# Attention scores in a two-layer decoder trunk: heads paired over the array's two row halves, masks added on VectorE

## The chip, the cores and the metric

The kernel runs on one core of one Trainium2 chip. The metric is device time in microseconds, the median of several runs. The kernel before takes 1220.24 us (three runs, 1218.81 to 1221.25).

## What is computed

The reference is a two-layer decoder trunk on x of shape (1, 256, 1024) in float32. Each layer is a half SwiGLU block, a token mixer, cross-attention into 256 memory tokens, and another half SwiGLU block, each with its RMS norm and residual. What matters here are the scores of the token mixers. All heads have 64 dimensions, and the 256 tokens are two blocks of 128.

```python
# layer 0, band heads (8 query heads, 2 key heads): scores, distance bias, band mask, a sink in the softmax
s = einsum(q, k) * dh ** -0.5
s = where(valid, s + bias, -inf); m = maximum(max(s), sink)
p = exp(s - m); o = (p / (sum(p) + exp(sink - m))) @ v
# layer 0, stick-breaking heads (8): no softmax
z = einsum(q, k) * scale
log_keep = where(strict, log_sigmoid(-z), 0)
a = where(strict, exp(log_sigmoid(z) + cumsum_after(log_keep)), 0); o = a @ v
# layer 1, dilated heads (16): three dilation patterns mixed, which one softmax does
# over s + bias, where the bias holds the slope and the log of how often a key counts
```

## The kernel before, in words

The program is one stream written in order: for each layer FFN, mixer, cross-attention, FFN. Nearly all work on TensorE (PE) is matrix products of activations with weights. Each weight tile is loaded from HBM by SP's queue (`raw`, L170 and L172), rounded to a high part on ScalarE (`wh`, L174) and subtracted to a low part on VectorE (`wl`, L176), and each product is then three matmuls (`mm3`, L181 to L183; in the FFN's wide form L318 and L319). The pools hold 4 raw tiles, 10 tiles of weight parts (five pairs), 10 work tiles of 128x512 (`wk`), 6 PSUM banks for products (`mm`) and 2 for transposes (`tp`).

The small work of attention is put between those products by a planner in Python. `later(delay, fn)` puts a step on a heap with a due time; each product calls `tick(ns)` with its supposed cost, which advances the planner's clock and then starts at most one step that is due. A step's own tick advances the clock too, but starts nothing. `need(tag)` starts all steps of that tag that are left. The delays stand in `LAG`. The framework then schedules the instructions by priority (the order written) and readiness, so an instruction can move past one that would not be ready, and it gives each tile a free buffer of its pool; an engine runs its queue in the order so made.

Three places make scores:

- **Band heads**, `even_mixer`'s `scores` (L572) called from `attend` (L443). Groups are of four heads for the first block of queries (128 keys) and of two heads for the second (256 keys), six groups: (0,0), (0,4), (1,0), (1,2), (1,4), (1,6). Heads 0 to 3 lie on partitions 0 to 63 of `qaT` and `kaT`, heads 4 to 7 on partitions 64 to 127. Each head's slice of the bank gets the bias table by a bfloat16 matmul with an identity over all 128 rows (L580), and then the product of 64 rows (L582, float32, which runs as two passes of weight load and matmul). VectorE reduces the maxima from PSUM (L587, L589), ScalarE makes the exponentials from PSUM into a work tile (L455), 7.5 us of the planner later four transposes (L207) and a copy (L461) follow, and then the products with values (L603). Between these steps stand the products that make the stick-breaking queries and keys (`ws_blocks`, L306).
- **Stick-breaking heads**, `stick(h)` (L674), one head after another with a gap of 1900 ns. A bfloat16 matmul over all rows writes the mask of 384 columns (L679); two float32 products of 64 rows with 256 and 128 columns are added to it (L680, L682). Even heads lie on the lower half of the partitions, odd heads on the upper half. ScalarE makes abs, exp and log (L686 to L688), VectorE and ScalarE the parts of the log sums (L692 to L697), and 3200 ns of the planner after the scores `after` sums them on PE (L704 to L706); then L708, L709, and 1000 ns later the products with values (L717 to L719). Between these steps stands the projection of the memory's keys (`mem.keys`, 96 matmuls of 512 columns).
- **Dilated heads**, `odd_mixer`'s `scores` (L786), twelve groups: four of four heads with 128 keys, then eight of two heads with 256 keys. Each group loads its bias table into a work tile (L794), makes products of 64 rows (L800), and VectorE adds bank and table in place (L804). Then come L807, L455 and, 17.6 us of the planner later, the transposes. All heads of one group lie on one half of the partitions (`hf`). The projection of the values and of the memory's keys stand between.

Of the kernel before, what the change touches and what calls it, by code (L numbers as in the profile page):

```python
# [13 lines left out]
BF16 = mybir.dt.bfloat16  # L14
AF = mybir.ActivationFunctionType
ALU = mybir.AluOpType
AX = mybir.AxisListType

P = 128
# [19 lines left out]
def kernel(  # L39
# [95 lines left out]
    ident_b = const.tile([P, P], BF16, name="ident_b")  # L135
    nc.vector.tensor_copy(ident_b, ident)
# [10 lines left out]
    def psum():  # L147
        return mm.tile([P, 512], F32, name="mm")
# [371 lines left out]
    def even_mixer(w_in, q_gain, k_gain, sinks, w_out, next_vec, mem, first=False):  # L520
# [18 lines left out]
        def evac_qk(t, pq, pk):  # L539
# [17 lines left out]
            def turn():  # L557
# [5 lines left out]
                if t == 1:  # L563
                    attend([(0, 0), (0, 4), (1, 0), (1, 2), (1, 4), (1, 6)], scores, values, LAG['band_gap'], LAG['band_p'],
                           first=1500.0, tag="band")
# [5 lines left out]

        def scores(grp):  # L572
# [3 lines left out]
            ps = psum()  # L576
            for i in range(per):
                hf, b = (h0 + i) // 4, (h0 + i) % 4
                sl = ps[:, i * keys:(i + 1) * keys]
                nc.tensor.matmul(sl, lhsT=ident_b, rhs=bband[:, h0 + i, 2 * P - keys:2 * P],  # L580
                                 start=True, stop=False)
                nc.tensor.matmul(sl, lhsT=qaT[hf * 64:(hf + 1) * 64, b, t * P:(t + 1) * P],  # L582
                                 rhs=kaT[hf * 64:(hf + 1) * 64, 0:keys], start=False, stop=True)
            tick(1100)
            s = blocks(ps, keys)
# [5 lines left out]
            return s, nm, dn[t][:, h0:h0 + per], None  # L591
# [81 lines left out]

        def stick(h):  # L674
            hs = slice((h % 2) * 64, (h % 2) * 64 + 64)
            b = h // 2
            ps = psum()
            z = ps[:, 0:384]
            nc.tensor.matmul(z, lhsT=ident_b, rhs=smask, start=True, stop=False)  # L679
            nc.tensor.matmul(ps.rearrange("p (a t) -> p a t", t=256)[:, :, 0:128],  # L680
                             lhsT=kbT[hs, b, 0:P], rhs=qbT[hs, b, :], start=False, stop=False)
            nc.tensor.matmul(ps[:, 128:256], lhsT=kbT[hs, b, P:2 * P], rhs=qbT[hs, b, P:2 * P],  # L682
                             start=False, stop=True)
            tick(830)
# [53 lines left out]
    def odd_mixer(w_in, q_gain, k_gain, w_out, next_vec, mem):  # L738
# [45 lines left out]

        if True:
            def scores(grp):  # L786
# [6 lines left out]
                tab = work()  # L793
                nc.sync.dma_start(blocks(tab, keys), dil_bias[:, h0:h0 + per, 256 - keys:256])  # L794
                ps = psum()
# [218 lines left out]
```

## Time and profile before

| | |
|---|---|
| median of three runs | 1220.24 us (1218.81 to 1221.25) |
| the profiled execution's own time | 1220.4 us |
| its span, first to last instruction | 1218.6 us |
| instructions | 17064 |
| TensorE clock granted over the span | 1.00 (2.4 GHz) |

The rows in a later section come from that one execution. PE is TensorE's matmuls, PEld its weight loads, DVE is VectorE, ACT ScalarE, POOL GpSimd, SP the engine whose queue issues the DMAs. Starts and durations in a timeline are microseconds from the first instruction; rows of like instructions next to each other are merged, with their count behind the x, and the duration is then that from the first start to the last end. A matmul's duration includes its way through the array, so matmuls overlap in the rows, and what one takes of the engine's time is read from start to start. A form like 64*128 128x256 is 64 rows by 128 columns of weights; the last number is how many columns are streamed.

### The profile page before, as it was taken

Reading aid. Unit: us, or ns where it says so; the run is one execution under the profiler, and the core shown is the slowest. Engines: PE = TensorE matmul, PEld = TensorE weight load, DVE = VectorE, ACT = ScalarE, POOL = GpSimd, SP = SyncE. Lnnn points to the kernel's source line nnn. Section 1 sums busy time; section 2 is a strip of 40 time slices with the busy share of each in tenths; the row PEclk is TensorE's granted clock in tenths of the full one; section 3 lists DMA queues with packets and bytes.
Section 4 is the critical chain, followed back from the end, with each engine's and each line's share of the span. In section 5 each row is a group of like instructions: output and inputs, shape, how many; then the busy total and the mean of one; then the engine's idle time right before and its main releaser. Section 6 shows DMA issues by size and latency. Waiting matters only on the chain.

```text
span 1218.6 us, 17064 instructions
## 1 busy us (share of the span) xinstructions
PE 1209.0 (99%) x6390; PEld 1023.5 (84%) x6390; DVE 762.2 (63%) x979; ACT 648.1 (53%) x1078; POOL 63.8 (5%) x123
## 2 busy tenths in 40 slices
PE   8999999999999999999999999999999999999998
PEld 7888888887888888888888888888788888888887
DVE  6666645665766676665376675376666776667651
ACT  6656534646655565555365554265643654656540
POOL 1000000200010000000000000033000100000000
PEclk9999999999999999999999999999999999999999
DMA  8765664731444485666385657346634545665560
GB/s 261 248 193 176 220 210 136 257 107 35 138 161 143 141 272 171 195 207 207 104 259 174 207 191 263 117 155 202 204 113 139 189 145 158 222 202 178 182 199 35
DMA packets 136756, 216.71 MB, mean 178 GB/s; under 512 B 10337, under 2 KB 104161, under 8 KB 136674
## 3 DMA queue, kind: packets, MB, share of 16 engines
q1 hardware_dynamic: 136674, 215.63, 54.5%
q8 instruction: 50, 0.82, 0.3%
q14 instruction: 32, 0.26, 0.1%
HBM read 214.54 MB, written 1.05 MB: 177 GB/s over the span
## 4 chain that ended last, share of the span: by engine, by line
PE 95%; DVE 1%; DMA 1%; ACT 1%; issue 0%; POOL 0%; SPq 0%; ACTq 0%; POOLq 0%; DVEq 0%
PE mm L318 22%; PE mm L181 18%; PE mm L182 17%; PE mm L183 17%; PE mm L319 12%; PE tp L207 3%; PE mm L800 1%; DMA raw<-in_xa_w_o_dram 1%; PE mm L821 1%; DVE wl L176 1%; PE mm L582 1%; PE mm L300 1%; DMA x<-in_x_dram 0%; PE mm L603 0%; PE mm L680 0%
## 5 line engine op out<-in xcount | busy, mean ns | idle before, releaser
L176 DVE TENSOR_TENSOR wl<-raw,wh 128x1024 fp32r<-128x1024 f32 x386 | 463.7, 1220 | 145.2 <-ACT wh L174 143.8
L174 ACT CAST wh<-raw 128x1024 fp32r<-128x1024 f32 x386 | 394.0, 1051 | 156.2 <-PE mm L183 80.0
L318 PE MATMUL mm<-xs,wh 128*128 128x512 f32 x1184 | 413.7, 394 | 0.0
L319 PE MATMUL mm<-xs,wl 128*128 128x256 f32 x1184 | 331.8, 280 | 0.0
L318 PEld LDWEIGHTS mm<-xs,wh 128*128 128x128 f32 x1184 | 221.8, 187 | 50.4
L319 PEld LDWEIGHTS mm<-xs,wl 128*128 128x128 f32 x1184 | 223.8, 189 | 0.0
L181 PE MATMUL mm<-wh,big 128*128 128x512 f32 x480 | 193.3, 403 | 0.0
L183 PE MATMUL mm<-wh,big 128*128 128x512 f32 x480 | 187.4, 390 | 0.0
L182 PE MATMUL mm<-wl,big 128*128 128x512 f32 x480 | 187.3, 390 | 0.0
L181 PE MATMUL mm<-wh,xs 128*128 128x512 f32 (+1 forms) x432 | 171.9, 398 | 0.0
L182 PE MATMUL mm<-wl,xs 128*128 128x512 f32 (+1 forms) x432 | 167.6, 388 | 0.0
L183 PE MATMUL mm<-wh,xs 128*128 128x512 f32 (+1 forms) x432 | 167.3, 387 | 0.0
L322 ACT COPY wk<-mm 128x256 f32<-128x256 f32 x148 | 55.3, 374 | 152.0 <-PE mm L319 151.6
L323 DVE TENSOR_TENSOR wk<-mm,wk 128x256 f32<-128x256 f32 x148 | 62.3, 421 | 96.9 <-ACT wk L322 96.9
L181 PEld LDWEIGHTS mm<-wh,big 128*128 128x128 f32 x480 | 90.3, 188 | 19.3 <-issue 2.0
L183 PEld LDWEIGHTS mm<-wh,big 128*128 128x128 f32 x480 | 90.1, 188 | 19.2
L182 PEld LDWEIGHTS mm<-wl,big 128*128 128x128 f32 x480 | 90.4, 188 | 15.9
L183 PEld LDWEIGHTS mm<-wh,xs 128*128 128x128 f32 x432 | 81.2, 188 | 16.5
L181 PEld LDWEIGHTS mm<-wh,xs 128*128 128x128 f32 x432 | 81.3, 188 | 15.2 <-issue 0.3
L182 PEld LDWEIGHTS mm<-wl,xs 128*128 128x128 f32 x432 | 81.4, 188 | 14.3
L207 PE MATMUL tp<-ident,wk 128*128 128x128 f32 x376 | 56.7, 273 | 0.8 <-DVE wk L440 0.8
L207 PEld LDWEIGHTS tp<-ident,wk 128*128 128x128 f32 x376 | 46.0, 141 | 12.4 <-issue 1.6
(159 smaller groups left out, 959.6 us busy)
## 6 DMA issues: line engine op xcount, KB each, us to landing
raw<-in_ffn_w_gu_dram SPq DMA_DIRECT2D x344, 256.0 KB, 4.2
raw<-in_ffn_w_down_dram SPq DMA_DIRECT2D x88, 512.0 KB, 4.4
raw<-in_xa_w_kv_dram SPq DMA_DIRECT2D x32, 512.0 KB, 5.4
raw<-in_od_w_in_dram SPq DMA_DIRECT2D x24, 512.0 KB, 4.4
raw<-in_ev_w_in_dram SPq DMA_DIRECT2D x18, 512.0 KB, 4.5
raw<-in_xa_w_q_dram SPq DMA_DIRECT2D x16, 512.0 KB, 4.6
raw<-in_xa_w_o_dram SPq DMA_DIRECT2D x16, 512.0 KB, 4.3
raw<-in_ev_w_out_dram SPq DMA_DIRECT2D x8, 512.0 KB, 3.8
```

Of the source, the lines that this page charges most:

```text
L174: nc.scalar.copy(wh, r)
L176: nc.vector.tensor_tensor(wl, r, f32(wh), op=ALU.subtract)
L181: nc.tensor.matmul(ps, lhsT=a[0], rhs=b[0], start=start, stop=False)
L182: nc.tensor.matmul(ps, lhsT=a[0], rhs=b[1], start=False, stop=False)
L183: nc.tensor.matmul(ps, lhsT=a[1], rhs=b[0], start=False, stop=stop)
L207: nc.tensor.transpose(ps[:, b * P:(b + 1) * P], src[:, b * P:(b + 1) * P], ident)
L300: nc.tensor.matmul(ps[:, b * 256:(b + 1) * 256], lhsT=w[k // per][x][:, o:o + P], rhs=xboth(k)[y], start=i == 0 and k == 0, stop=i == 2 an ...
L318: nc.tensor.matmul(ps, lhsT=wh, rhs=xs[:, :, :, k, :], start=k == 0, stop=False)
L319: nc.tensor.matmul(ps[:, 0:256], lhsT=wl, rhs=xh[:, :, k, :], start=False, stop=k == NK - 1)
L322: nc.scalar.copy(part[:, bs], ps[:, 256:512])
L323: nc.vector.tensor_tensor(out[:, bs], ps[:, 0:256], part[:, bs], op=ALU.add)
L582: nc.tensor.matmul(sl, lhsT=qaT[hf * 64:(hf + 1) * 64, b, t * P:(t + 1) * P], rhs=kaT[hf * 64:(hf + 1) * 64, 0:keys], start=False, stop=True)
```

## The change

Heads are scored in pairs of groups, one group on each half of the partitions. The products of the two groups alternate between the halves, head by head, and go to two PSUM banks. A float32 product stays two passes, so passes run lower, lower, upper, upper, and so on. The pair is made when its first group comes up, and the second group then starts with the reduction. The orders of groups are changed so that partners follow each other.

For band heads the identity matmuls (16) go; VectorE adds bank and bias table into a work tile, once for each group (6 of 128x512), and the later steps read that work tile. For stick-breaking heads the mask matmuls (8) go; two heads are scored together and VectorE adds the mask, once for each head (8 of 128x384); z is then read from a work tile. For dilated heads nothing is added or removed on VectorE; the two groups' tables are loaded together. The ticks change: a pair now costs the planner 1000, 800 and 1000 ns, where two groups cost 2200, 1660 and 1780. The identity in bfloat16 goes.

```diff
--- before.py
+++ after.py
@@ -132,8 +132,6 @@
             nc.sync.dma_start(xres[t][:, cs], x_in[0, t * P:(t + 1) * P, cs])
     ident = const.tile([P, P], F32, name="ident")
     make_identity(nc, ident)
-    ident_b = const.tile([P, P], BF16, name="ident_b")
-    nc.vector.tensor_copy(ident_b, ident)
     mhalf = const.tile([P, 16], F32, name="mhalf")
     nc.gpsimd.memset(mhalf, -0.5)
     neg_1 = const.tile([P, P], F32, name="neg_1")
@@ -561,34 +559,43 @@
                 ps = transpose4(qn)
                 nc.vector.tensor_scalar(qaT[:, :, t * P:(t + 1) * P], blocks(ps), g[:, 0:1], None, op0=ALU.mult)
                 if t == 1:
-                    attend([(0, 0), (0, 4), (1, 0), (1, 2), (1, 4), (1, 6)], scores, values, LAG['band_gap'], LAG['band_p'],
+                    attend([(0, 0), (0, 4), (1, 0), (1, 4), (1, 2), (1, 6)], scores, values, LAG['band_gap'], LAG['band_p'],
                            first=1500.0, tag="band")
             later(LAG['rsband'], scale, "band")
 
         nm8 = [sm.tile([P, 8], F32, name="nm8") for _ in range(2)]
         dn = [sm.tile([P, 8], F32, name="dn") for _ in range(2)]
         po_a = [None, None]
+
+        paired = {}
 
         def scores(grp):
             t, h0 = grp
             keys = (t + 1) * P
             per = 512 // keys
-            ps = psum()
-            for i in range(per):
-                hf, b = (h0 + i) // 4, (h0 + i) % 4
-                sl = ps[:, i * keys:(i + 1) * keys]
-                nc.tensor.matmul(sl, lhsT=ident_b, rhs=bband[:, h0 + i, 2 * P - keys:2 * P],
-                                 start=True, stop=False)
-                nc.tensor.matmul(sl, lhsT=qaT[hf * 64:(hf + 1) * 64, b, t * P:(t + 1) * P],
-                                 rhs=kaT[hf * 64:(hf + 1) * 64, 0:keys], start=False, stop=True)
-            tick(1100)
-            s = blocks(ps, keys)
+            if h0 < 4:
+                two = [psum(), psum()]
+                for i in range(per):
+                    for hf in range(2):
+                        rows = slice(hf * 64, hf * 64 + 64)
+                        nc.tensor.matmul(two[hf][:, i * keys:(i + 1) * keys],
+                                         lhsT=qaT[rows, h0 + i, t * P:(t + 1) * P], rhs=kaT[rows, 0:keys],
+                                         start=True, stop=True)
+                tick(1000)
+                for hf in range(2):
+                    h = h0 + 4 * hf
+                    tab = work()
+                    nc.vector.tensor_tensor(blocks(tab, keys), blocks(two[hf], keys),
+                                            bband[:, h:h + per, 2 * P - keys:2 * P], op=ALU.add)
+                    paired[t, h] = tab
+            tab = paired[grp]
+            s = blocks(tab, keys)
             m = sm.tile([P, 8], F32, name="mx")
             nc.vector.tensor_reduce(out=m[:, 0:per], in_=s, axis=AX.X, op=ALU.max)
             nm = nm8[t][:, h0:h0 + per]
             nc.vector.scalar_tensor_tensor(nm, in0=m[:, 0:per], scalar=-1.0, in1=nsink[:, h0:h0 + per],
                                            op0=ALU.mult, op1=ALU.min)
-            return s, nm, dn[t][:, h0:h0 + per], None
+            return s, nm, dn[t][:, h0:h0 + per], tab
 
         def values(grp, pt):
             t, h0 = grp
@@ -671,17 +678,24 @@
         ob = [work() for _ in range(2)]
         po = [None]
 
+        zs = [None, None]
+
         def stick(h):
-            hs = slice((h % 2) * 64, (h % 2) * 64 + 64)
             b = h // 2
-            ps = psum()
-            z = ps[:, 0:384]
-            nc.tensor.matmul(z, lhsT=ident_b, rhs=smask, start=True, stop=False)
-            nc.tensor.matmul(ps.rearrange("p (a t) -> p a t", t=256)[:, :, 0:128],
-                             lhsT=kbT[hs, b, 0:P], rhs=qbT[hs, b, :], start=False, stop=False)
-            nc.tensor.matmul(ps[:, 128:256], lhsT=kbT[hs, b, P:2 * P], rhs=qbT[hs, b, P:2 * P],
-                             start=False, stop=True)
-            tick(830)
+            if h % 2 == 0:
+                two = [psum(), psum()]
+                rows = [slice(0, 64), slice(64, 128)]
+                for ps, hs in zip(two, rows):
+                    nc.tensor.matmul(ps.rearrange("p (a t) -> p a t", t=256)[:, :, 0:128],
+                                     lhsT=kbT[hs, b, 0:P], rhs=qbT[hs, b, :], start=True, stop=False)
+                for ps, hs in zip(two, rows):
+                    nc.tensor.matmul(ps[:, 128:256], lhsT=kbT[hs, b, P:2 * P], rhs=qbT[hs, b, P:2 * P],
+                                     start=False, stop=True)
+                tick(800)
+                for i in range(2):
+                    zs[i] = work()
+                    nc.vector.tensor_tensor(zs[i][:, 0:384], two[i][:, 0:384], smask, op=ALU.add)
+            z = zs[h % 2][:, 0:384]
             e = work()
             nc.scalar.activation(e[:, 0:384], z, AF.Abs)
             nc.scalar.activation(e[:, 0:384], e[:, 0:384], AF.Exp, scale=-1.0)
@@ -782,6 +796,8 @@
                 for fn in waiting[t]:
                     fn()
 
+        paired = {}
+
         if True:
             def scores(grp):
                 t, h0 = grp
@@ -790,18 +806,24 @@
                 per = 512 // keys
                 need(f"q{t}")
                 need(f"k{t}")
-                tab = work()
-                nc.sync.dma_start(blocks(tab, keys), dil_bias[:, h0:h0 + per, 256 - keys:256])
-                ps = psum()
-                for i in range(per):
-                    h = h0 + i
-                    hf, b = (h % 8) // 4, h % 4
-                    hs = slice(hf * 64, hf * 64 + 64)
-                    nc.tensor.matmul(ps[:, i * keys:(i + 1) * keys],
-                                     lhsT=qT[hh][hs, b * 256 + t * P:b * 256 + (t + 1) * P],
-                                     rhs=kT[hh][hs, b * 256:b * 256 + keys], start=True, stop=True)
-                tick(890)
-                nc.vector.tensor_tensor(tab, ps, tab, op=ALU.add)
+                if h0 % 8 < 4:
+                    two = [psum(), psum()]
+                    tabs = [work(), work()]
+                    for hf in range(2):
+                        h = h0 + 4 * hf
+                        nc.sync.dma_start(blocks(tabs[hf], keys), dil_bias[:, h:h + per, 256 - keys:256])
+                    for i in range(per):
+                        for hf in range(2):
+                            hs = slice(hf * 64, hf * 64 + 64)
+                            b = h0 % 4 + i
+                            nc.tensor.matmul(two[hf][:, i * keys:(i + 1) * keys],
+                                             lhsT=qT[hh][hs, b * 256 + t * P:b * 256 + (t + 1) * P],
+                                             rhs=kT[hh][hs, b * 256:b * 256 + keys], start=True, stop=True)
+                    tick(1000)
+                    for hf in range(2):
+                        nc.vector.tensor_tensor(tabs[hf], two[hf], tabs[hf], op=ALU.add)
+                        paired[t, h0 + 4 * hf] = tabs[hf]
+                tab = paired[grp]
                 s = blocks(tab, keys)
                 nm = sm.tile([P, 4], F32, name="nm")
                 nc.vector.tensor_reduce(out=nm[:, 0:per], in_=s, axis=AX.X, op=ALU.max, negate=True)
@@ -833,7 +855,7 @@
         project(lambda k: w_in[k * P:(k + 1) * P, 0:1024], xparts, evac_qk(qT, True, "q"), tags=("x0", "x1"))
         tc.keep_in_program_order(nc.scalar.preload_act_table_set("exp_and_others"))
         project(lambda k: w_in[k * P:(k + 1) * P, 1024:2048], xparts, evac_qk(kT, False, "k"))
-        groups = [(t, h) for t in range(2) for h in range(0, 16, 4 // (t + 1))]
+        groups = [(0, 0), (0, 4), (0, 8), (0, 12)] + [(1, h + o) for h in (0, 8) for o in (0, 4, 2, 6)]
         attend(groups, scores, values, LAG['att_gap'], LAG['att_p'], first=LAG['att_first'], tag="att", ready=with_v)
         project(lambda k: w_in[k * P:(k + 1) * P, 2048:3072], xparts, evac_v)
         mem.keys()
```

## Rows read from the trace of the kernel before

**Rows 1.** The page, parts 1 and 4: busy time by engine, the chain that ended last.

```profile
PE 1209.0 (99%) x6390; PEld 1023.5 (84%) x6390; DVE 762.2 (63%) x979; ACT 648.1 (53%) x1078; POOL 63.8 (5%) x123
...
PE 95%; DVE 1%; DMA 1%; ACT 1%; issue 0%; POOL 0%; SPq 0%; ACTq 0%; POOLq 0%; DVEq 0%
```

**Rows 2.** Busy time by stretch: PE, PEld, DVE, ACT, POOL, clock, DMA share, GB/s.

```profile
241.60:272.80 31.20, 31.20 (x214) 25.77 (x214) 20.56 (x34) 15.90 (x44) 0.00 (x0) 1.00 0.35 113
272.80:320.00 47.20, 47.20 (x266) 38.21 (x264) 28.84 (x52) 30.67 (x68) 2.93 (x6) 1.00 0.13 39
```

**Rows 3.** Timeline (start, us, engine, line), PE, around a first-block band group.

```profile
241.56 0.28 PE L183 MATMUL mm<-xs,wl 128*128 128x256 f32 x1
241.68 0.23 PE L580 MATMUL mm<-big,ident_b 128*128 128x128 bf16 x1
...
244.21 0.28 PE L182 MATMUL mm<-xs,wh 128*128 128x256 f32 x1
```

**Rows 4.** Timeline, PE, around one stick-breaking head.

```profile
272.60 0.39 PE L182 MATMUL mm<-wl,big 128*128 128x512 f32 x1
272.83 0.40 PE L183 MATMUL mm<-wh,big 128*128 128x512 f32 x1
...
273.33 0.70 PE L680 MATMUL mm<-big 64*128 64x256 f32 x2
273.87 0.38 PE L682 MATMUL mm<-big 64*128 64x128 f32 x2
...
274.52 0.40 PE L182 MATMUL mm<-wl,big 128*128 128x512 f32 x1
```

**Rows 5.** Timeline, PE, around a second-block band group.

```profile
252.68 0.28 PE L183 MATMUL mm<-xs,wl 128*128 128x256 f32 x1
...
254.71 0.28 PE L182 MATMUL mm<-xs,wh 128*128 128x256 f32 x1
```

**Rows 6.** Timeline, PE, around a first-block dilated group.

```profile
849.48 0.39 PE L183 MATMUL mm<-wh,xs 128*128 128x512 f32 x1
849.80 1.16 PE L800 MATMUL mm<-big 64*128 64x128 f32 x8
...
851.23 0.39 PE L182 MATMUL mm<-wl,xs 128*128 128x512 f32 x1
```

**Rows 7.** Timeline, PE, around a second-block dilated group.

```profile
870.58 0.39 PE L183 MATMUL mm<-wh,xs 128*128 128x512 f32 x1
...
872.29 0.40 PE L182 MATMUL mm<-wl,xs 128*128 128x512 f32 x1
```

**Rows 8.** Groups by line and shape: count, busy us, mean ns, idle before.

```profile
L804 DVE TENSOR_TENSOR wk<-mm,wk 128x512 f32<-128x512 f32 x12 | 8.2, 684 | 5.1 <-PE mm L800 4.2 <-DMA wk<-in_dil_bias_dram 0.9
...
L800 PEld LDWEIGHTS mm<-big 64*128 64x128 f32 x64 | 9.2, 186 | 4.7 <-issue 2.9 <-ACT wk L455 0.4 <-DVE nm L807 0.4
...
L708 DVE TENSOR_TENSOR wk<-mm,wk 128x384 f32<-128x384 f32 x8 | 4.4, 555 | 3.2 <-PE mm L706 3.2
```

**Rows 9.** Timeline, weight loads of the two dilated groups.

```profile
849.80 0.96 PEld L800 LDWEIGHTS mm<-big 64*128 64x128 f32 x8 [0.35 <-ACT wh L174]
...
870.89 0.73 PEld L800 LDWEIGHTS mm<-big 64*128 64x128 f32 x4 [0.35 <-issue]
```

**Rows 10.** Timeline, all engines, two stretches of the stick-breaking stage.

```profile
280.74 0.65 PE L207 MATMUL tp<-ident,big 128*128 128x128 f32 x4
281.02 0.56 DVE L695 TENSOR_TENSOR wk<-wk 128x384 fp32r<-128x384 f32 x1 [0.58 <-ACT wk L694]
...
282.71 0.34 PE L705 MATMUL mm<-wk,neg_ur 128*128 128x384 f32 x1
...
289.05 0.55 DVE L695 TENSOR_TENSOR wk<-wk 128x384 fp32r<-128x384 f32 x1
...
292.53 0.34 PE L705 MATMUL mm<-wk,neg_ur 128*128 128x384 f32 x1
```

**Rows 11.** Waits of SP's own queue, whole span: total us, times, longest.

```profile
SPq L794 <- PE tp L207: 12.7, 3, 10.8
```

## The prediction, as it went on record before the change was run

> **What bounds the kernel now.** I read the page's busy shares and its chain first: TensorE is busy 99% of the span and makes up 95% of the chain [rows 1]. So TensorE time that goes is gained almost in full, and work on other engines is free as long as nothing that TensorE needs comes later. Busy time by stretch says how much room there is. In the band stretch VectorE works 20.56 of 31.20 us, in the stick-breaking stretch 28.84 of 47.20, TensorE all of both [rows 2]. Then I priced each visit to the scores from start to start, since matmul durations overlap.
>
> A visit costs the time from the L183 before it to the L182 behind it, less the ordinary spacing of the two products that frame it: 0.12 us with 256 columns (241.56 to 241.68) [rows 3], 0.23 us with 512 columns (272.60 to 272.83) [rows 4].
> - band, first block, 4 heads: 244.21 - 241.56 - 0.24 = 2.41 us [rows 3]; two groups
> - band, second block, 2 heads: 254.71 - 252.68 - 0.24 = 1.79 us [rows 5]; four groups
> - stick-breaking, one head: 274.52 - 272.83 - 0.46 = 1.23 us [rows 4]; eight heads
> - dilated, first block, 4 heads: 851.23 - 849.48 - 0.46 = 1.29 us [rows 6]; four groups
> - dilated, second block, 2 heads: 872.29 - 870.58 - 0.46 = 1.25 us [rows 7]; eight groups
>
> The sum is 4.8 + 7.2 + 9.8 + 5.2 + 10.0 = 37.0 us. The change can act on no more than that, 3% of the span.
>
> **What a visit is made of.** One load takes 186 ns [rows 8]. Eight loads with 128 columns streamed take 0.96 us, so they follow each other at (0.96 - 0.19) / 7 = 0.11 us; four with 256 columns take 0.73 us, which is 0.11 for the first step and (0.73 - 0.19 - 0.11) / 2 = 0.215 for the later ones [rows 9]. So a pass costs 0.11 us at 128 columns and 0.215 at 256, and a load that nothing hides costs 0.11. The rest is fixed: 1.29 - 8 x 0.11 = 0.41, and 1.25 - 4 x 0.215 = 0.39. I take 0.40 us for leaving the full array and coming back, two ways of about 0.20; the loads' engine stands idle 0.35 us before such a visit [rows 9].
>
> **The change part by part.** *Matmuls removed and visits merged* have one price. If the two halves run strictly in turn, a pair costs 0.40 + 16 x 0.11 = 2.16 us (first block), 0.40 + 8 x 0.215 = 2.12 (second block), 0.40 + 4 x 0.215 + 4 x 0.11 = 1.70 (two stick-breaking heads). With 3, 6 and 4 such pairs that is 6.5 + 12.7 + 6.8 = 26.0 us, a saving of 11.0.
>
> *Two halves at once* has no row: nowhere before do products of the two halves stand next to each other. Bounds: no overlap saves 11.0 as above; complete overlap of the halves gives 0.40 + 0.88, 0.40 + 0.86 and 0.40 + 0.65, together 3.8 + 7.6 + 4.2 = 15.6 us, a saving of 21.4. A loss has its place under the rivals. Passes are issued lower, lower, upper, upper, so in order only the second pass of one half can lie beside the first of the other: 8 passes take 5 places, 16 take 9. The nearest row is that of the loads: they come 0.11 us apart whatever is streamed. If loads of both halves still pass one at a time, a pass of 128 columns gains nothing, since a load fills it, and one of 256 does. Then first-block pairs stay at 2.16, second-block pairs cost 0.40 + 5 x 0.215 = 1.48, stick-breaking pairs 0.40 + 3 x 0.215 + 2 x 0.11 = 1.27: 6.5 + 8.9 + 5.1 = 20.4 us. I take this value, **16.6 us saved**. If loads of both halves overlap too, first-block pairs fall to 0.40 + 9 x 0.11 = 1.39 and 18.9 us are saved.
>
> *Adds on VectorE.* Six of 128x512 at 684 ns and eight of 128x384 at 555 ns, from the nearest adds of a bank and a work tile [rows 8]: 4.1 + 4.4 = 8.5 us of VectorE, hidden under TensorE. In the band stretch VectorE then has 24.7 us in 31.2 - (12.0 - 5.1) = 24.3 us, so there it is full. The Trainium skill's page "TensorEngine Tiling (Array Packing)", section "PSUM Bottleneck", warns of this: tiling makes TensorE faster, not the emptying of PSUM, which can then be the limit. By that rule the band stretch would end 0.4 us later than my sum, no more. Without it the same follows from the rows, and the stretch behind has room: 33.2 of about 42.5 us. I count it in the term for waits.
>
> *Longer chains.* The add stands between scores and ScalarE. In the stick-breaking stage the first head's sums wait least: L695 ends at 281.58 and the matmul that reads it starts at 282.71, 1.1 us later; a later head has 292.53 - 289.60 = 2.9 us [rows 10]. In between stands the next head's visit of 1.23 us, which moves forward to the first of its pair. An add of 0.56 us and its hand-over (0.1) come in. The first head so lacks 0.8 us; later ones keep 2.9 - 1.23 - 0.7 = 1.0. For the second head of a pair the chain is shorter, its z being ready. Band groups wait 7.5 us of the planner before their transposes; dilated chains don't grow. 0.8 us is taken.
>
> *Buffers and queues.* Pairs hold z or the second table one gap longer in the 10 work tiles, but free their banks at the add. SP's queue shows that the tiles are scarce already: its table loads waited 12.7 us for transposes to release one, 10.8 us at the longest, with weight loads queued behind [rows 11]. Five pairs of weight parts cover that: each feeds four steps of three matmuls, 5 x 4 x 0.69 = 13.8 us. A pair that asks for two tiles may wait one gap more (about 5 us): 10.8 + 5 - 13.8 = 2.0 us of stall at most, nothing at least. I take 0.7, as the nearest row shows no stall. The planner's clock now moves less per pair, as TensorE does, and each stage's chain ends earlier against the filler. Tables are still 12 loads. The identity's copy at the start lies beside the first loads: nothing.
>
> **The sum.** 16.6 - 0.8 - 0.7 = 15.1 us less. The rows are of an execution of 1220.4 us with a span of 1218.6; it lies 0.16 above the median of 1220.24, and what surrounds the span stays. 1220.4 - 15.1 - 0.2 = **1205.1 us**.
>
> **Rivals.**
> *Halves in turn, no overlap.* For it: no row shows two halves at once, and the scheduler can put other work into a pair, as it put four transposes between the two products of one head [rows 10]. Against: nothing but their order links the halves. It keeps the merged visits: 1220.2 - 11.0 + 1.5 = 1210.7 us. This is also the case in which the change doesn't do what it says. Chance 0.26.
>
> *Complete overlap.* Each half would run as an array of its own, with its loads, and the order in pairs of passes would cost nothing. For it: separate rows, separate banks. Against: loads at 0.11 us each, one after another [rows 9], and queues in order. It saves 21.4: 1220.2 - 21.4 + 1.5 = 1200.3 us; with overlap in order and loads side by side 1220.2 - 18.9 + 1.5 = 1202.8. Chance of the two 0.18. The Trainium skill's page "TensorEngine Tiling (Array Packing)", section "Theoretical Speedup", gives up to twofold for a contraction of 64 rows, which is this rival's first number; no run here shows it yet.
>
> *A turn between halves costs like a change of shape (slower).* A pair of first-block groups turns 7 times, every other pair 3 times: 3 x 7 + 10 x 3 = 51 turns. If each cost a way of 0.20 us, 10.2 of the 11.0 us would go: 1220.2 - 11.0 + 10.2 + 1.5 = 1220.9, no change. If each cost leaving and entering, 0.40 us, it would be 1220.2 - 11.0 + 20.4 + 1.5 = 1231.1. It decides from (11.0 - 1.5 + 2.4) / 51 = 0.23 us per turn. For it: the full array's change to 64 rows and back is paid at every visit [rows 3, 4]. Against: both halves have one form, 64*128, and eight passes with weights of four heads pay nothing between them [rows 9]. The same page's "Key Properties" says that a change of mode drains the engine, a change of tile alone does not; by that sentence this rival falls. Chance 0.04 for no change, 0.06 for slower.
>
> *Waits eat the gain.* If full work tiles stretch the stick-breaking chain, TensorE runs out of filler. If that stage stayed at its 47.2 us [rows 2], the 9.8 - 5.1 = 4.7 us gained there would be lost: 1205.1 + 4.7 = 1209.8 us. Chance 0.04, on top of any of these.
>
> **How the numbers follow.** The forecast has 0.42, and the cases above 0.26, 0.18, 0.10 and 0.04. The time is that of the likeliest. The range goes from complete overlap (1200.3, a little less without its waits) to halves in turn with the full stall of 2.0 us (1220.2 - 11.0 + 0.8 + 2.0 = 1212.0, and 1 us for rounding in the bounds): **1199.8 to 1213.0 us**; outside are the turns that cost and a part of the rest. A difference of 0.2% (2.4 us) is about what a measurement can tell from no change. Faster by more than that: 0.87. Within: 0.06. Slower: 0.07.
>
> **What would show it.** Groups L580 and L679 are gone; 14 new adds stand on VectorE at 0.55 to 0.69 us. The visit to a second-block pair takes about 1.5 us by the same reckoning (2.1 if in turn, 1.3 if complete), a first-block pair 2.2 (1.4 if loads overlap), a stick-breaking pair 1.3. Starts of matmuls of the two halves lie close together where they overlap; a gap of 0.2 us at each turn would show the slower rival. TensorE stays at 99%; a wait of TensorE for VectorE or a work tile of over 2 us in sum would prove my terms for waits wrong, and a visit outside 1.3 to 2.2 us my account of the array.

## The result, and the profile after

The changed kernel takes 1205.74 us (median of four runs, 1204.01 to 1208.18), the kernel before 1219.93 us beside it: 0.9885 of it, with a 95% interval of 0.9863 to 0.9906. The forecast was 1205.1. The profiled execution took 1207.32 us with a span of 1205.6; against the one of before (1220.4) that is 13.1 us less.

The page's busy times and its chain by engine, changed kernel, beside [rows 1]:

```profile
PE 1192.6 (99%) x6366; PEld 1011.7 (84%) x6366; DVE 766.6 (64%) x992; ACT 646.1 (54%) x1078; POOL 63.5 (5%) x123
...
PE 92%; DVE 3%; DMA 2%; ACT 1%; issue 1%; POOL 0%; SPq 0%; ACTq 0%; DVEq 0%; POOLq 0%
```

TensorE is still the bound at 99%, but VectorE now has 3% of the chain: there are waits that were not there.

To see where time went I took landmarks, the start of the same product's last matmul in both traces (all products with weights stand in the same order): the ends of the products around the even layer's attention, around the second FFN of layer 0, and around the odd layer's attention. The two attention stretches, landmark to landmark (start:end and length, then busy us and instructions of PE, PEld, DVE, ACT and POOL, granted clock, DMA share, GB/s), before:

```profile
240.48:331.25 90.77, 90.77 (x542) 74.42 (x541) 58.67 (x95) 53.67 (x123) 3.86 (x8) 1.00 0.29 93
829.72:938.82 109.10, 109.10 (x576) 87.93 (x575) 71.60 (x93) 56.60 (x131) 12.05 (x19) 1.00 0.50 164
```

and after:

```profile
238.91:321.46 82.55, 81.74 (x518) 68.96 (x517) 64.64 (x109) 53.23 (x123) 3.95 (x8) 1.00 0.32 101
821.75:925.62 103.87, 102.19 (x577) 83.88 (x575) 70.85 (x93) 56.04 (x132) 12.05 (x19) 1.00 0.52 173
```

The even layer (band and stick-breaking) gives 90.77 - 82.55 = 8.2 us, the odd one (dilated) 5.2. The rest is not the change's: this execution reached the first landmark 1.6 us earlier, and its second FFN of layer 0 took 1.9 us more (last section).

Now the visits. TensorE's timeline, changed kernel: a band first-block pair (8 heads), a band second-block pair (4 heads) and a dilated second-block pair:

```profile
239.99 0.28 PE L181 MATMUL mm<-xs,wl 128*128 128x256 f32 x1
240.19 1.16 PE L581 MATMUL mm<-big 64*128 64x128 f32 x16
...
241.51 0.28 PE L180 MATMUL mm<-xs,wh 128*128 128x256 f32 x1
...
247.17 0.28 PE L181 MATMUL mm<-xs,wl 128*128 128x256 f32 x1
247.38 1.13 PE L581 MATMUL mm<-big 64*128 64x256 f32 x8
...
248.67 0.28 PE L180 MATMUL mm<-xs,wh 128*128 128x256 f32 x1
...
860.04 0.39 PE L181 MATMUL mm<-wh,xs 128*128 128x512 f32 x1
860.36 1.13 PE L819 MATMUL mm<-big 64*128 64x256 f32 x8
...
861.76 0.40 PE L180 MATMUL mm<-wl,xs 128*128 128x512 f32 x1
```

By the prediction's own reckoning they cost 241.51 - 239.99 - 0.24 = 1.28 us, 248.67 - 247.17 - 0.24 = 1.26 and 861.76 - 860.04 - 0.46 = 1.26. One dilated group alone cost 1.29 and 1.25 [rows 6, 7]: the second group is free. The weight loads say the same. PEld's timeline, a dilated first-block and a second-block pair:

```profile
841.83 0.97 PEld L819 LDWEIGHTS mm<-big 64*128 64x128 f32 x16 [0.35 <-ACT wh L172]
...
860.36 0.73 PEld L819 LDWEIGHTS mm<-big 64*128 64x128 f32 x8 [0.35 <-ACT big L793]
```

Sixteen loads now take the time of eight, and eight that of four [rows 9]; in the records a pass of the upper half starts 6 to 7 ns after that of the lower. All three band visits cost 3.8 us (12.0 before), all six dilated ones 7.6 (15.2 before).

The adds on VectorE, by form (line, engine, operation, tiles, count, then busy us and mean ns, then idle time before them):

```profile
L697 DVE TENSOR_TENSOR wk<-mm,smask 128x384 f32<-128x384 f32 x8 | 4.0, 547 | 0.0
...
L588 DVE TENSOR_TENSOR wk<-mm,big 128x512 f32<-128x512 f32 x6 | 3.8, 680 | 0.6 <-PE mm L581 0.6
```

They have the prices taken (684 and 555 ns). The stick-breaking pairs are another matter. TensorE's timeline, the first of them:

```profile
265.32 0.40 PE L181 MATMUL mm<-wh,big 128*128 128x512 f32 x1
265.64 0.70 PE L689 MATMUL mm<-big 64*128 64x256 f32 x2
266.27 1.10 PE L610 MATMUL mm<-big,wk 128*128 128x64 f32 x8
267.30 0.70 PE L689 MATMUL mm<-big 64*128 64x256 f32 x2
267.93 1.10 PE L610 MATMUL mm<-big,wk 128*128 128x64 f32 x8
268.96 0.49 PE L692 MATMUL mm<-big 64*128 64x128 f32 x4
...
269.73 0.40 PE L180 MATMUL mm<-wl,big 128*128 128x512 f32 x1
```

The scheduler put full-array products with values (L610) inside the pair, so the halves stand apart and the change of shape is paid three times. In the later pairs the sums of an earlier head (L718 to L720) do the same; in the fourth the second head became a visit of its own. All four are split: about 2.2, 1.9, 1.9 and 2.5 us, 8.5 in all against 9.8 before. (The work inside is taken off at what it costs elsewhere: 0.11 us a pass of L610, 0.57 us for a head's sums.)

Waits. TensorE in the odd attention stretch (line waited for, then us in total, times, longest), changed kernel:

```profile
PE mm L843 <- ACT wh L172: 0.9, 1, 0.9
PE tp L205 <- DVE wk L438: 0.7, 1, 0.7
```

The first one on VectorE's timeline and on TensorE's:

```profile
864.49 1.28 DVE L824 TENSOR_TENSOR wk<-mm,wk 128x512 f32<-128x512 f32 x2
865.69 0.67 DVE L829 TENSOR_REDUCE nm<-wk 128x2 f32<-128x512 f32 x1
866.28 0.68 DVE L459 COPY wk<-tp 128x512 f32<-128x512 f32 x1
```

```profile
867.10 1.08 PE L843 MATMUL mm<-big,wk 128*128 128x64 f32 x8 [0.86 <-ACT wh L172]
```

The rows name ScalarE's L172, but what L843 reads is the copy of the transposes, L459, which ends at 866.96. It stood on VectorE's queue behind both adds of the pair and a reduction, one add more than a single group puts there.

The second wait has one more cause in it. VectorE's timeline of that pair, from its first add to L438, which scales the attention's output before TensorE transposes it:

```profile
873.49 0.69 DVE L824 TENSOR_TENSOR wk<-mm,wk 128x512 f32<-128x512 f32 x1 [0.67 <-DMA wk<-in_dil_bias_dram]
...
877.02 0.68 DVE L438 TENSOR_TENSOR wk<-mm,rd 128x512 f32<-128x512 f32 x1
```

The first add waited 0.67 us for its bias table, and from there to the end of L438 VectorE had no pause. Ten of the eleven other traces with dilated pairs have the same: VectorE waits 0.5 to 1.1 us for that table, and TensorE then 0.5 to 2.6 us for the operation that is L438 here. In the eleventh (halves not in turn) the table is in time and TensorE still waits 0.5 us, so the late table is a part of that wait and not all of it; no run loads the tables sooner.

From start to start the odd stretch has stalls of 1.03, 0.88 and 0.29 us, the even one of 0.88 (a transpose that waits for VectorE's L188 behind the band adds) and 0.26: 3.3 us in all, 2.8 of them waits for VectorE. VectorE in the band stretch alone (columns as above), beside the first window of [rows 2], is all but full:

```profile
240.19:265.30 25.11, 24.40 (x209) 22.98 (x209) 23.65 (x44) 16.72 (x46) 0.00 (x0) 1.00 0.40 126
```

On SP's queue another table load, for a later pair, waited longest, for a work tile that L438 had to release (compare [rows 11]). TensorE lost nothing by that one: the pair's first add then waited for its products and not for a table.

```profile
SPq L814 <- DVE wk L438: 10.3, 1, 10.3
```

### The profile page after: what moved, and what is told of

Same layout as the page of the kernel before. It is cut to its first block, busy times and chain, and to the rows that moved or that the text cites. A ratio compares the mean times of both kernels' runs of the same rounds, so it can differ in the third digit from the quotient of the medians.

```text
span 1205.6 us, 17032 instructions
## 1 busy us (share of the span) xinstructions
PE 1192.6 (99%) x6366; PEld 1011.7 (84%) x6366; DVE 766.6 (64%) x992; ACT 646.1 (54%) x1078; POOL 63.5 (5%) x123
## 3 DMA queue, kind: packets, MB, share of 16 engines
HBM read 214.54 MB, written 1.05 MB: 179 GB/s over the span
## 4 chain that ended last, share of the span: by engine, by line
PE 92%; DVE 3%; DMA 2%; ACT 1%; issue 1%; POOL 0%; SPq 0%; ACTq 0%; DVEq 0%; POOLq 0%
PE mm L316 23%; PE mm L179 17%; PE mm L180 17%; PE mm L181 17%; PE mm L317 12%; PE tp L205 3%; DVE wl L174 1%; DMA raw<-in_xa_w_o_dram 1%; PE mm L843 1%; ACT wh L172 1%; PE mm L610 0%; DMA x<-in_x_dram 0%; PE mm L689 0%; DVE big L188 0%; PE mm L298 0%
## 5 line engine op out<-in xcount | busy, mean ns | idle before, releaser
L172 ACT CAST wh<-raw 128x1024 fp32r<-128x1024 f32 x386 | 394.3, 1051 | 164.6 <-PE mm L181 81.7
```

The source lines that it names most:

```text
L172: nc.scalar.copy(wh, r)
```

## The experiments

Theory: both halves run at once, their loads too; band and dilated visits give all of it, the stick-breaking part gives little because its pairs are split and its chains are longer, and VectorE's queue takes some back. Rivals: the order in turns is what makes them overlap, or the gain is that of the removed mask matmuls; and in the stick-breaking stage the due times, not the adds, are what costs. Each run is told by its ratio to the kernel before on the same chip and by the landmarks: by how much the even and the odd attention stretch of its profiled execution differ from before.

| run | median us | ratio (95%) | even, us | odd, us |
|---|---|---|---|---|
| the change | 1205.74 | 0.9885 (0.9863 to 0.9906) | -8.2 | -5.2 |
| halves not in turn | 1207.67 | 0.9895 (0.9865 to 0.9925) | -8.5 | -5.4 |
| masks on VectorE only | 1223.53 | 1.0023 (1.0013 to 1.0034) | +3.5 | 0.0 |
| dilated pairs only | 1214.63 | 0.9955 (0.9939 to 0.9972) | 0.0 | -5.0 |
| stick-breaking sums later | 1210.14 | 0.9915 (0.9894 to 0.9937) | -3.7 | -5.1 |
| dilated adds one by one | 1209.83 | 0.9913 (0.9898 to 0.9927) | -8.2 | -4.4 |
| stick-breaking as before | 1207.51 | 0.9891 (0.9874 to 0.9908) | -7.1 | -5.1 |
| pairs sooner, sums later | 1205.48 | 0.9876 (0.9859 to 0.9893) | -9.5 | -5.1 |
| the same again | 1206.91 | 0.9883 (0.9861 to 0.9906) | -9.5 | -4.9 |
| nine work tiles | 1209.96 | 0.9914 (0.9898 to 0.9929) | -4.8 | -5.2 |
| stick-breaking masks by matmul | 1203.88 | 0.9864 (0.9842 to 0.9886) | -10.7 | -5.4 |
| that, pairs sooner | 1205.53 | 0.9871 (0.9853 to 0.9890) | -10.0 | -5.3 |
| the change again | 1206.87 | 0.9884 (0.9864 to 0.9903) | -8.2 | -5.5 |

**Halves not in turn.** All products of one half, then all of the other (band, stick-breaking and dilated alike).

```diff
-                for i in range(per):
-                    for hf in range(2):
+                for hf in range(2):
+                    for i in range(per):
```

> The pairs stay, but each pair issues all products of the lower half and then all of the upper half. Theory A (the halves run at the same time when they alternate): each visit then costs the passes of both halves one after the other, 2.1 to 2.2 us for a band or dilated pair where the change takes 1.26 to 1.29, 1.7 for a stick-breaking pair that isn't split; 3 x 0.88 + 6 x 0.86 + 4 x up to 0.65 = 8 to 10 us slower than the change, about 1214 to 1216 us. Theory B (fewer visits and no mask matmuls are the gain, the order within a pair is nothing): as the change, 1205 to 1207 us.

The ratio cannot be told from the change's, so the order hardly matters to the time. TensorE's timeline of this kernel, a band first-block and a dilated second-block pair:

```profile
241.80 0.28 PE L181 MATMUL mm<-xs,wl 128*128 128x256 f32 x1
242.01 1.71 PE L581 MATMUL mm<-big 64*128 64x128 f32 x16
...
243.87 0.28 PE L180 MATMUL mm<-xs,wh 128*128 128x256 f32 x1
...
860.65 0.39 PE L181 MATMUL mm<-wh,xs 128*128 128x512 f32 x1
860.97 1.14 PE L818 MATMUL mm<-big 64*128 64x256 f32 x8
...
862.38 0.40 PE L180 MATMUL mm<-wl,xs 128*128 128x512 f32 x1
```

The 16 passes cost 243.87 - 241.80 - 0.24 = 1.83 us, between 1.28 (in turn) and 2.16 (one after another); the upper half's first pass starts at 242.57, when five of the lower half's eight have started. The 8 passes cost 862.38 - 860.65 - 0.46 = 1.27, as in turn, though all of the lower half's four were issued first. TensorE thus starts passes of the free half ahead of passes issued earlier for the busy one: three of those were passed over in either pair. Turns shorten only the long pair, and its 0.55 us show in neither stretch because the stalls were shorter in this run (the band stage's 0.33 us in place of 0.88, and none at the products with values in the odd layer).

**Masks on VectorE only.** The kernel before with the new adds of band and stick-breaking heads, no pairs.

```diff
-                nc.tensor.matmul(sl, lhsT=ident_b, rhs=bband[:, h0 + i, 2 * P - keys:2 * P],
-                                 start=True, stop=False)
...
+            tab = work()
+            nc.vector.tensor_tensor(blocks(tab, keys), blocks(ps, keys),
+                                    bband[:, h0:h0 + per, 2 * P - keys:2 * P], op=ALU.add)
...
+            zt = work()
+            nc.vector.tensor_tensor(zt[:, 0:384], ps[:, 0:384], smask, op=ALU.add)
```

> Only the masks of band and stick-breaking heads go to VectorE; no pairs, dilated heads as before. Theory A: band visits fall from 2.41 and 1.79 to about 1.28 and 1.26 us (2 x 1.13 + 4 x 0.53 = 4.4 us), stick-breaking heads from 1.23 to 1.05 (8 x 0.18 = 1.4 us), together 5.8 us less TensorE time, minus some waits: 1214 to 1216 us. Theory B: most of the 14 us is here, 1208 us or less.

Slower than before. The band visits fell as they should, to 1.28 us (four heads) and 1.25 (two heads), 7.6 us in all: 4.4 of the 8.2 us that the band part gains are the removed bias matmuls, 3.8 the pairing. But the even stretch as a whole is 3.5 us longer, so what follows the band visits lost 3.5 + 4.4 = 7.9 us. TensorE's waits in it, and the stretch that came soon after the stall of 0.8 us:

```profile
PE mm L717 <- ACT wk L709: 2.0, 1, 2.0
PE mm L704 <- ACT wk L723: 1.1, 1, 1.1
PE mm L704 <- ACT wk L694: 0.8, 1, 0.8
```

```profile
295.00:298.50 3.50, 3.50 (x10) 2.74 (x10) 1.58 (x3) 2.29 (x5) 0.00 (x0) 0.53 0.02 5
```

After a stall of 0.8 us in a stretch of small products the granted clock was 0.53 for 3.5 us (1.2 of 2.4 GHz): about half of them lost once more. Other work also split four of the eight heads' visits. VectorE was not full there (33.1 of 52.7 us, from 265.3 to 318.0). An add and a work tile per head in that chain cost more than the mask matmuls, which are worth 1.23 - 1.05 = 0.18 us a visit (a whole visit to one head cost 1.05 here). Which of the two, the add or the tile, costs more this run does not show.

**Dilated pairs only.** The kernel before with the changed `odd_mixer`.

```diff
+                if h0 % 8 < 4:
+                    two = [psum(), psum()]
+                    tabs = [work(), work()]
...
-        groups = [(t, h) for t in range(2) for h in range(0, 16, 4 // (t + 1))]
+        groups = [(0, 0), (0, 4), (0, 8), (0, 12)] + [(1, h + o) for h in (0, 8) for o in (0, 4, 2, 6)]
```

> Only the dilated heads are paired; band and stick-breaking heads as before. No matmul is removed here. Theory A: two visits of 1.28 and 1.26 us become one of the same length, so 2 x 1.28 + 4 x 1.26 = 7.6 us less TensorE time, of which the two waits of about 1 us each seen in the changed kernel are given back: 1214 to 1216 us by the time, and about 5.2 us gained between the landmarks of this stage. Theory B: six visits fewer at 0.40 us, 2.4 us minus the same waits: 1218 to 1220 us.

The odd stretch gives 5.0 us and the even one nothing: the dilated gain does not depend on the rest, and with no matmul removed it is the pairing's. Six visits fewer at 0.40 us would have given 2.4.

**Stick-breaking sums later.** 4500 instead of 3200 ns between the scores and the sums, so that no earlier head's sums are due at a pair.

```diff
-    "put": 400, "stick_gap": 1900, "stick_u": 3200, "stick_v": 1000, "stick_o": 1300, "head64": 7000,
+    "put": 400, "stick_gap": 1900, "stick_u": 4500, "stick_v": 1000, "stick_o": 1300, "head64": 7000,
```

> The change with the planner's delay from stick-breaking scores to their sums 4500 ns in place of 3200, which leaves three of the four stick-breaking pairs whole in TensorE's queue instead of none. Theory C (a split pair runs its halves in turn and pays the change of shape twice): each whole pair falls from about 1.9 to 2.2 us to 1.05, so 2.5 to 3 us less than the change, 1203 us. Rival: the sums come later and the stage's end waits for them, so no gain or a loss of 1 to 3 us.

Three of four pairs stay whole and cost 1.05 us for two heads, which is 0.40 + 0.65, the price of complete overlap. But the stage ends later. TensorE's timeline at its end, and the granted clock behind it:

```profile
310.73 0.69 PE L731 MATMUL mm<-big,wk 128*128 128x64 f32 x2 [4.15 <-ACT wk L723]
```

```profile
306.60:310.70 4.10, 0.00 (x0) 0.00 (x0) 3.58 (x4) 3.85 (x9) 1.58 (x2) 0.86 0.93 338
310.70:316.40 5.70, 5.67 (x17) 4.89 (x18) 4.21 (x8) 1.43 (x2) 0.00 (x0) 0.50 0.84 282
```

The filler is used up before the last head's chain is through: 4.1 us without a matmul, and then 5.7 us at half the clock. The stretch loses 4.5 us to the change.

**Pairs sooner, sums later.** To keep pairs whole without that end, the gap between heads goes to 700 ns as well. Run twice.

```diff
-    "put": 400, "stick_gap": 1900, "stick_u": 3200, "stick_v": 1000, "stick_o": 1300, "head64": 7000,
+    "put": 400, "stick_gap": 700, "stick_u": 4500, "stick_v": 1000, "stick_o": 1300, "head64": 7000,
```

> The change with the gap between stick-breaking heads 700 ns in place of 1900 and the delay to the sums 4500 in place of 3200: three of four pairs whole, and the chain started sooner against the filler. Theory C2 (the later sums lost their gain because the last heads came after the filler had run out): 2 to 3 us less than the change, 1203 us, TensorE waits in that stage under 1 us. Rival (VectorE and ScalarE can't keep up with closer heads): waits of several us, 1206 us or more.

> Whole pairs sooner (gap 700, delay 4500) once more beside the change: 1.2 us less than it between the landmarks of the even layer's attention, so 1 us less in the median, which these rounds can only just tell.

The even stretch gives 9.5 us both times, 1.3 more than the change. By the ratios, whose intervals overlap with the change's, no difference is shown.

**Dilated adds one by one.** The second group's add waits for its own turn, to shorten the queue in front of L459 and L438.

```diff
-                        nc.vector.tensor_tensor(tabs[hf], two[hf], tabs[hf], op=ALU.add)
-                        paired[t, h0 + 4 * hf] = tabs[hf]
-                tab = paired[grp]
+                        paired[t, h0 + 4 * hf] = two[hf], tabs[hf]
+                ps, tab = paired[grp]
+                nc.vector.tensor_tensor(tab, ps, tab, op=ALU.add)
```

> The change, but each dilated group's add of bank and table is made when that group comes up, not both adds when the pair is scored; the second bank stays taken for one gap. Theory E (a pair's two adds of 0.68 us stand on VectorE ahead of the copies and scalings that TensorE waits for): the waits of about 1.0 and 0.9 us in the dilated stage go, 1 to 2 us less than the change, 1204 us, and the stage gains 6.5 to 7.5 us in place of 5.2. Rival (those waits come from other work, or a bank held longer makes new ones): the stage gains 5.2 us or less.

It helped half way. The stall of 1.03 us at the products with values (L843) is gone, as theory E has it. But the one for L438 grew to 2.6 us, and the stretch gains 0.8 us less than in the change. VectorE's timeline, the first add in front of that L438:

```profile
878.36 0.69 DVE L826 TENSOR_TENSOR wk<-mm,wk 128x512 f32<-128x512 f32 x1 [1.08 <-DMA wk<-in_dil_bias_dram]
```

It waited 1.08 us for its table, longer than in the change, and a copy, a reduction and L438 stand right behind it. Why the table came later here, and whether the bank that is held longer has a part in it, is not shown.

**Stick-breaking as before.** The change with `stick` and its mask matmuls put back.

```diff
-            if h % 2 == 0:
-                two = [psum(), psum()]
...
+            nc.tensor.matmul(z, lhsT=ident_b, rhs=smask, start=True, stop=False)
```

> The change without its stick-breaking part: band and dilated heads paired, the stick-breaking masks by matmuls, head by head, as before. Theory D (split pairs and longer chains leave the stick-breaking part no net gain): the even layer's attention gains the same 8.2 us as in the change, and the time is the change's within 2 us, 1204 to 1208 us. Rival (that part brings the 4.7 us of the forecast): 1209 to 1211 us, and 3 to 4 us between the landmarks.

The even stretch gives 7.1 us without any stick-breaking part: that part is worth 1.2 us, by these two executions, close to the 1.3 us that its visits save.

**Nine work tiles.**

```diff
-    wk = ctx.enter_context(tc.tile_pool(name="wk", bufs=10))
+    wk = ctx.enter_context(tc.tile_pool(name="wk", bufs=9))
```

> The change with 9 work tiles in place of 10. Theory F (work tiles are what the longer chains run out of): the waits grow, 2 to 8 us slower than the change, most of it in the two attention stages. Rival (there are enough of them): as the change, 1204 to 1207 us.

The even stretch gets 3.4 us worse, all of it in the stick-breaking stage (stalls of 0.56 and 1.9 us, and a clock of 0.72 over the 6 us that hold the second); the odd one stays. So with nine, work tiles bind where z takes one per head, and not where two tables are loaded at once. More than ten were not tried.

**Stick-breaking masks by matmul.** Pairs, but each bank gets the mask first by the identity matmul, and ScalarE reads z from PSUM; no add, no work tile. The second bank comes from the transposes' pool.

```diff
-                two = [psum(), psum()]
+                two = [psum(), tps()]
...
+                for ps in two:
+                    nc.tensor.matmul(ps[:, 0:384], lhsT=ident_b, rhs=smask, start=True, stop=False)
...
-                for i in range(2):
-                    zs[i] = work()
-                    nc.vector.tensor_tensor(zs[i][:, 0:384], two[i][:, 0:384], smask, op=ALU.add)
+                zs[:] = two
```

> The change, but the stick-breaking pairs get their masks by matmul again (one per bank, before the pair's products), so z stays in PSUM and no add and no work tile is spent on it; the second bank comes from the transposes' pool. Theory D2 (in the stick-breaking stage the add and the work tile cost what the removed matmul gives): a whole pair takes 0.32 us of masks + 0.1 + 1.05 = 1.5 us against 2 x 1.23 before, and no chain grows: the even layer's attention gains 9 to 11 us in place of 8.2, 1203 to 1205 us. Rival (masks on VectorE are worth having in that stage): 7 to 8 us between the landmarks, 1206 us or more.

With it ran the same kernel with pairs sooner and sums later (700 and 4500 ns, the edit above), and the change itself once more:

> As the run before, with the gap of 700 ns and the delay of 4500. Theory D2: as the run before or up to 1 us less. Rival: banks held from scores to the last use of z make waits once heads come closer, some us more.

> The change itself once more, beside the others of this call: 1204 to 1208 us; between the landmarks of the even layer's attention 8.2 us less than before and of the odd layer's 5.2, whatever the run; the pace of the wide products in the FFNs may differ by 1.8 us per stage.

TensorE's timeline of this kernel, its second pair:

```profile
276.12 0.40 PE L183 MATMUL mm<-wh,big 128*128 128x512 f32 x1
276.36 0.34 PE L691 MATMUL mm<-smask,ident_b 128*128 128x384 bf16 x1
276.53 0.33 PE L691 MATMUL tp<-smask,ident_b 128*128 128x384 bf16 x1
276.79 0.48 PE L693 MATMUL mm<-big 64*128 64x256 f32 x1
276.79 0.48 PE L693 MATMUL tp<-big 64*128 64x256 f32 x1
...
277.64 0.51 PE L181 MATMUL mm<-wh,big 128*128 128x512 f32 x1
277.98 0.39 PE L182 MATMUL mm<-wl,big 128*128 128x512 f32 x1
```

277.98 - 276.12 - 0.46 = 1.40 us for two heads, masks included; two heads cost 2.46 before. Three of four pairs stay whole at the old due times, and no wait over 0.24 us is left in the stage. The shorter chain, whose sums are ready sooner, would explain that; but the second bank comes from another pool here too, and no run separates the two. The even stretch gives 10.7 us, where the change gave 8.2 in both of its executions. It is the fastest kernel measured, 3.0 us below the change on the same chip; the two ratios' intervals overlap, so the medians alone do not show it. With pairs sooner it gains nothing more.

## Why the prediction was right, and where not

The time came out right (1205.1 against 1205.74), but not by the terms that were forecast, and that it came so close is luck. The choice on the two halves took away 21.4 - 16.6 = 4.8 us that complete overlap gives. Four whole stick-breaking pairs would have saved 9.8 - 4.2 = 5.6 us with it; the split ones, which the sum did not have, saved 1.3, which is 4.3 less. The two errors nearly cancel.

- *Two halves at once.* The choice that loads of both halves pass one at a time was wrong. The rival "complete overlap" holds: pairs cost 1.28, 1.26 and (whole, in the run with later sums) 1.05 us, where it says 1.28, 1.26 and 1.05. Band and dilated visits so save 8.2 + 7.6 = 15.8 us; the terms taken come to 12.0 - 5.1 + 15.2 - 10.2 = 11.9. The row that led there, loads 0.11 us apart [rows 9], was one of a single half. The Trainium skill's page "TensorEngine Tiling (Array Packing)", section "Theoretical Speedup", gives up to twofold for 64 rows, and the trace agrees: 16 loads in 0.97 us where 8 took 0.96.
- *Visits merged, stick-breaking.* 4.7 us were expected, 1.3 came. The rival on turns had named that the scheduler can put other work into a pair [rows 10]; the sum took the pairs as whole.
- *Longer chains* (0.8 us) and *buffers and queues* (0.7 us): 1.5 expected, 3.3 measured as stalls; the 2.8 us of them that wait for VectorE are over the 2 us that the prediction set as its own mark. "Dilated chains don't grow" is the step that failed: a pair puts two adds on VectorE's queue at once, and what TensorE waits for stands behind them. With the adds one by one the stall of 1.03 us is gone. A stall through SP's queue did come, but not the one that was worked out: TensorE did not run out of weights behind a table load, even when one waited 10.3 us; a late table held up VectorE by 0.67 us in front of the stall of 0.88. The cover against the first was counted too small, here and in the words on the kernel: high and low parts have ten tiles each, so ten pairs and not five.
- *Adds on VectorE.* Prices right, and the band stretch is as full as worked out: 23.65 us of VectorE in 25.11, forecast 24.7 in 24.3. It cost one stall of 0.88 us. The same page of the Trainium skill, section "PSUM Bottleneck", says that the emptying of PSUM can become the limit; here the trace agrees for that stretch, to that amount. In the stick-breaking stage of the run with masks only VectorE had room, and 7.9 us were lost there all the same, so the harm lay in the longer chain, its work tiles or both.
- *A turn costs like a change of shape.* Wrong: 6 to 7 ns from half to half.
- *Waits eat the gain.* This rival, given 0.04, had the right stage but not the way: there 1.2 us of the 4.7 were left, yet the change's stalls in that stage were under 0.5 us, and the rest went with the split pairs. Stalls, the lower clock behind them and split visits made masks alone slower.

In sum: visits -8.2 - 1.3 - 7.6 = -17.1, stalls +3.3, so -13.8 us against the forecast's -15.1. The two stretches together gave 13.4, the medians differ by 14.2.

## What to carry to other kernels

Two products of 64 rows on the two row halves cost TensorE what one costs, loads included, so pair whatever uses half the rows, and look in the trace whether the pair was kept whole. Moving work from a busy TensorE to VectorE is not free because VectorE has idle time: ask which chain gets one step longer and what stands behind the new step in its queue. Here the matmul that writes a mask (0.18 us) was cheaper than the add that replaced it (0.55 us, a tile and a hand-over) in the chain that had no slack, by one execution against two of the change, and with the second bank from another pool.

## What the runs showed of the hardware that was not expected

Weight loads of the two halves run side by side, and passes of a free half start ahead of earlier ones of the busy half (above).

Two of the stretches behind stalls ran at the lower of TensorE's two levels, 1.2 of 2.4 GHz (granted clock 0.53 and 0.50 above): 5.7 us of it behind 4.1 us without a matmul, so by an estimate from that clock the stall cost half of 5.7, some 2.9 us, more than its length. The change's own stalls, 1 us at most, left the clock at 1.00.

The FFN's matmuls of 512 columns run at one of two paces, 230 or about 237 ns to the start of the next matmul, per stage and execution, at the same granted clock. The same 70 us of the second FFN of layer 0, before, changed kernel, and changed kernel again:

```profile
470.00:540.00 70.00, 70.00 (x406) 61.72 (x405) 45.38 (x62) 41.13 (x64) 0.00 (x0) 1.00 0.58 185
```

```profile
461.00:531.00 70.00, 70.00 (x399) 60.74 (x398) 44.59 (x62) 40.53 (x64) 0.00 (x0) 1.00 0.57 182
```

```profile
458.00:528.00 70.00, 70.00 (x405) 61.74 (x404) 44.83 (x63) 39.49 (x63) 0.00 (x0) 1.00 0.62 197
```

399 matmuls instead of 406 in 70 us, then 405 again with the same program: 1.9 us per stage that no edit explains. Two more executions, those of sums later and of adds one by one, had the slower pace in that stage. What sets the pace stayed open. It can move a median by more than some of the differences here, which is why the stretches stand beside the ratios.
